# Sums of weights formed in the recurrence and read back, and a fourth pair with seven products, in a decoder layer

## The chip, the cores and the metric

The kernel runs on one core of one Trainium2 chip. A core has a matrix engine (TensorE, in the profile PE, with its weight loads shown as PEld), three engines that work on elements (VectorE or DVE, ScalarE or ACT, GpSimd or POOL), and DMA engines that move data between DRAM and the on-chip memory. DMAs are issued by the queues of engines, here mostly by SyncE (SP), which does nothing else. TensorE writes to a small accumulation memory (PSUM), from which the element engines read.

The metric is the device time of one execution in microseconds (us). Before the change the median of three runs is 2254.96 us.

## The reference: what is computed

The reference is one decoder layer in float32 for 256 tokens of width 2048. In order:

```python
x = x + 0.5 * swiglu(rms_norm(x, ffn1_norm), ffn1_w_gate, ffn1_w_up, ffn1_w_down)   # width 5632
x = gated_parallel_mixer(x, ...)      # attention with sinks, beside an RWKV-7 recurrence
x = memory_cross_attention(x, mem, ...)
x = x + 0.5 * swiglu(rms_norm(x, ffn2_norm), ffn2_w_gate, ffn2_w_up, ffn2_w_down)
return rms_norm(x, final_norm)

def swiglu(h, w_gate, w_up, w_down):
    return (silu(h @ w_gate) * (h @ w_up)) @ w_down
```

The mixer takes all its projections out of one product with `w_in`. Its recurrence has 16 heads of size 64 and is sequential over the tokens; the kernel computes it in blocks of 128 tokens, by chains of small matmuls. Most of the time goes into products of the 256 tokens with weights that are read once from DRAM, some 400 MB.

## The kernel before, in words

**Products.** A float32 matmul is made of three matmuls on rounded operands: each operand is split into a high part (a ScalarE cast, `hi`) and a low part (what is left, a VectorE subtraction, `lo`), and the products high x high, high x low and low x high are added (`times`, lines 409 to 414). The weights come in units of two 128-row blocks by 512 columns. `load` (line 316) issues a unit's DMA on SP's queue into a buffer `raw`, `split_unit` (line 333) splits it.

**Eight products or seven.** In the feed-forward layers (from the second 512 columns on) two weight blocks are taken together, gate and up of the same columns. Two token halves times two weights times two blocks of K, called a pair q, make a 2 x 2 by 2 x 2 product of blocks: eight block products of three matmuls each. For the pairs in `SEVEN` (0, 2 and 4 of the eight pairs) the kernel uses the known scheme with seven products (p1 to p7 in `product_pair`, line 472). It needs sums of the activations (`combinations`, line 424; tiles `chi`, `clo`; four sums for each such pair, two for a plain pair ahead of the last one) and four sums of the weights, formed by four VectorE subtractions of 128 x 512 in `divide` (lines 366 to 369) and written to two `raw` buffers; the other operands are blocks of the weights as they are, so that an item with sums has one whole gate unit, half an up unit and two tiles of sums to split (`two_parts`, line 343, tiles `thi` and `tlo`, one buffer each for a and b).

**The order of the work.** `weight_plan` lists all products; their units form a list of items, one for each two blocks of K. `next_item` (line 373) hands out items, issues loads some units ahead (`LOADED`), and splits up to two units ahead (`AHEAD`); so for the paired items one item ahead. Items 0 to 139 are the first feed-forward layer, 140 to 379 the mixer and the cross-attention, the rest the second feed-forward layer.

All that isn't a product with weights is written as generators in groups of `Interleave` (line 52): attention, element work (`ew`), chains of the recurrence (two at a time), norms. A `tick` lets each of a group's first generators go one step. The loop of products calls a tick after each token half, so two for an item. The chains start behind item 267 and run beside the products with the gates of the recurrence (items 268 to 299); the product with `w_proj_rwkv` (items 300 to 315) reads their result `yr`. Each instruction goes to its engine's queue, which is worked off in order. `tc.issue_after` holds an instruction behind another one of the same engine.

**Memory.** The mixer's tiles of 4 KB per partition share a ring of `N4 = 22` buffers under the tag `t4`. The second feed-forward layer reuses the same memory: its `raw2` buffers (four, of two units each) take the loads of weights, and the four `raw` buffers then take sums.

## Time and profile before

| | |
|---|---|
| median of three runs | 2254.96 us (2254.9 to 2255.55) |
| profiled execution, its own time | 2254.95 us |
| its span, first to last instruction | 2253.2 us |
| TensorE busy | 2237.3 us, 10617 matmuls |
| VectorE busy | 1775.7 us |
| ScalarE busy | 1223.1 us |
| moved by DMA | 432.48 MB, mean 192 GB/s |
| granted TensorE clock | 0.999 |

How to read it: the shares are of the whole span, over stages that differ. The views by stretch show busy times in a window of the span. A row of the groups names line, engine, operation, result and operands, then shape and count, busy time and mean duration of one, and after a bar the idle time of that engine just before them and what ended it. In the list of waits, a row gives who waited for whom, the total, how often, and the longest one. In the timeline a row is start, duration, engine, line, operation. Matmuls overlap, so that a row's duration isn't what it takes in the stream; the distance between starts is.

### The profile page before, as it was taken

The page shows a single profiled execution, that of the slowest core. Times are in us where ns is not written, and L with a number is a line of the kernel's source. Part 1 is how long each engine was busy: PE and PEld are TensorE (multiplying, and loading weights), DVE is VectorE, ACT ScalarE, POOL GpSimd, SP SyncE. Part 2 cuts the span into 40 slices and gives each one's busy share as a digit, 9 for nine tenths or more (in the row PEclk, how much of TensorE's full clock was granted, in tenths as well). Part 3 has the DMA queues.
Part 4 walks back from the last instruction along what each step waited for, and adds up shares of the span by engine and source line. Part 5 has one row for each costly group of instructions (what it writes and reads, how often), then busy time and mean ns, then how long its engine had stood idle before and what let it go on. Part 6 is the DMA issues. An engine that isn't in the chain of part 4 may idle for free.

```text
span 2253.2 us, 28023 instructions
## 1 busy us (share of the span) xinstructions
PE 2237.3 (99%) x10617; PEld 1838.2 (82%) x10617; DVE 1775.7 (79%) x2273; ACT 1223.1 (54%) x1593; POOL 134.0 (6%) x192
## 2 busy tenths in 40 slices
PE   9999999999999999999999999999999999999998
PEld 7888888888888877788888888888888888888886
DVE  7898988998989476887534566547999988998987
ACT  6555555555556467444444446556555555554554
POOL 1000000000001000301220040001000000000002
PEclk9999999999999999999999999999999999999999
DMA  7565565556556545676533586558565565555564
GB/s 263 187 205 198 195 205 202 191 191 217 190 189 206 163 139 150 206 223 206 161 84 88 178 256 229 191 159 277 183 216 193 189 219 190 188 208 202 188 207 147
DMA packets 219142, 432.48 MB, mean 192 GB/s; under 512 B 14107, under 2 KB 16384, under 8 KB 219008
## 3 DMA queue, kind: packets, MB, share of 16 engines
q1 hardware_dynamic: 210432, 404.78, 54.7%
q0 software_dynamic: 8112, 25.12, 3.6%
q8 instruction: 83, 1.36, 0.3%
q10 hardware_dynamic: 464, 0.79, 0.1%
q14 instruction: 51, 0.42, 0.1%
HBM read 417.56 MB, written 13.11 MB: 191 GB/s over the span
## 4 chain that ended last, share of the span: by engine, by line
PE 47%; DVE 2%; DMA 1%; issue 0%; ACT 0%; POOLq 0%; POOL 0%; DVEq 0%; ACTq 0%
PE acc L412 9%; PE acc L414 9%; PE acc L413 9%; PE mm L414 4%; PE mm L413 4%; PE mm L412 4%; PE mm L1237 1%; PE tr L600 1%; PE tr L413 1%; PE tr L414 1%; PE tr L412 1%; DVE lo L340 1%; PE tr L1173 0%; DMA raw<-in_w_out_dram 0%; PE tr L1225 0%
## 5 line engine op out<-in xcount | busy, mean ns | idle before, releaser
L340 DVE TENSOR_TENSOR lo<-raw,hi 128x1024 fp32r<-128x1024 f32 (+1 forms) x770 | 894.2, 1163 | 345.6 <-ACT hi L339 343.9
L339 ACT CAST hi<-raw 128x1024 fp32r<-128x1024 f32 (+1 forms) x770 | 759.7, 997 | 736.1 <-PE acc L414 527.3
L412 PE MATMUL acc<-hi,xhi 128*128 128x512 f32 (+1 forms) x1196 | 476.4, 399 | 1.9 <-ACT xhi L627 1.4
L413 PE MATMUL acc<-lo,xhi 128*128 128x512 f32 (+1 forms) x1196 | 464.5, 388 | 0.0
L414 PE MATMUL acc<-hi,xlo 128*128 128x512 f32 (+1 forms) x1196 | 464.2, 389 | 0.0
L412 PEld LDWEIGHTS acc<-hi,xhi 128*128 128x128 f32 x1196 | 225.0, 188 | 52.2 <-issue 5.0
L414 PEld LDWEIGHTS acc<-hi,xlo 128*128 128x128 f32 x1196 | 224.4, 188 | 47.0 <-DVE xlo L628 1.0
L413 PEld LDWEIGHTS acc<-lo,xhi 128*128 128x128 f32 x1196 | 224.9, 188 | 46.2 <-issue 3.2
L347 ACT CAST thi<-raw 128x1024 fp32r<-128x1024 f32 x172 | 179.0, 1051 | 62.4 <-DVE raw L368 48.4
L348 DVE TENSOR_TENSOR tlo<-raw,thi 128x1024 fp32r<-128x1024 f32 x172 | 208.6, 1222 | 0.7 <-ACT thi L347 0.4
L412 PE MATMUL mm<-hi,xhi 128*128 128x512 f32 x380 | 149.3, 393 | 0.0
L414 PE MATMUL mm<-hi,xlo 128*128 128x512 f32 x380 | 148.1, 390 | 0.0
L413 PE MATMUL mm<-lo,xhi 128*128 128x512 f32 x380 | 148.1, 390 | 0.0
L413 PE MATMUL acc<-lo,hhi 128*128 128x512 f32 x372 | 145.5, 391 | 0.8 <-DVE lo L340 0.8
L414 PE MATMUL acc<-hi,hlo 128*128 128x512 f32 x372 | 145.5, 391 | 0.0
L412 PE MATMUL acc<-hi,hhi 128*128 128x512 f32 x372 | 144.9, 390 | 0.0
L414 PEld LDWEIGHTS mm<-hi,xlo 128*128 128x128 f32 x380 | 71.3, 188 | 15.0
L413 PEld LDWEIGHTS mm<-lo,xhi 128*128 128x128 f32 x380 | 71.4, 188 | 14.5
L412 PEld LDWEIGHTS mm<-hi,xhi 128*128 128x128 f32 x380 | 71.4, 188 | 14.5
L413 PEld LDWEIGHTS acc<-lo,hhi 128*128 128x128 f32 x372 | 69.9, 188 | 15.4 <-DVE lo L340 1.2
L412 PEld LDWEIGHTS acc<-hi,hhi 128*128 128x128 f32 x372 | 69.9, 188 | 14.3
L414 PEld LDWEIGHTS acc<-hi,hlo 128*128 128x128 f32 x372 | 69.9, 188 | 13.9
(384 smaller groups left out, 3500.6 us busy)
## 6 DMA issues: line engine op xcount, KB each, us to landing
raw<-in_ffn_w_up_dram SPq DMA_DIRECT2D x88, 1024.0 KB, 5.5
raw<-in_ffn_w_down_dram SPq DMA_DIRECT2D x88, 1024.0 KB, 5.2
raw<-in_ffn_w_gate_dram SPq DMA_DIRECT2D x84, 1024.0 KB, 5.2
raw<-in_w_in_dram SPq DMA_DIRECT2D x136, 512.0 KB, 3.7
raw<-in_w_out_dram SPq DMA_DIRECT2D x32, 512.0 KB, 4.6
raw<-in_w_proj_attn_dram SPq DMA_DIRECT2D x16, 512.0 KB, 4.1
raw<-in_w_proj_rwkv_dram SPq DMA_DIRECT2D x16, 512.0 KB, 5.4
raw<-in_w_cross_kv_dram SPq DMA_DIRECT2D x16, 512.0 KB, 4.0
```

The source lines that it names most:

```text
L339: at["hi"] = act.copy(hi[:, s], raw[:, s])
L340: at["lo"] = dve.tensor_tensor(lo[:, s], raw[:, s], f32(hi[:, s]), ALU.subtract)
L347: act.copy(hi[:], v[:])
L348: dve.tensor_tensor(lo[:], v[:], f32(hi[:]), ALU.subtract)
L412: pe.matmul(o, xh, hi, start=first, stop=False, **how)
L413: pe.matmul(o, xh, lo, start=False, stop=False, **how)
L414: pe.matmul(o, xl, hi, start=False, stop=last, **how)
L600: pe.transpose(b[:, o : o + P], tok[:, t, col : col + P], ident[:])
L1237: pe.matmul(vb[:, (o + k) * P : (o + k + 1) * P][:, r], lhs(k, e), rhs[:, k, r], start=first and k + e == 0, stop=True, **ek,)
```

## The change

In gate and up of the second feed-forward layer (`last`), pair 1 is taken in the seven-product form too: `SEVEN_2 = (0, 1, 2, 4)`. The weight sums of pairs 1 and 2 (`STAGED`) are no longer formed there. They are formed during the mixer, 20 times (two pairs of the ten products j = 1 to 10), by a new generator `stage` in a group of its own, four at a time: it waits for its position (`STAGE_AT`, items 255, 259, 263 and then 17 positions from 267 to 286), loads the four weight blocks into two `t4` tiles on SP's queue, lets four ticks pass, forms the sums in place in two steps of two VectorE subtractions each, lets six ticks pass, and stores the two tiles to DRAM (`sums`), on SP's queue too. In the second layer `load_sums` reads them back into `raw` buffers, up to two items ahead, and `divide` splits them. Of the up units in staged pairs, the block that only entered the sums isn't loaded; for that, some loads are cut into pieces.

The ring `t4` has 24 buffers instead of 22. To make room, the constants `bdup` and `center` move from the constant pool into the mixer's, `keep` takes the place of `ups`, and a smaller tile fills the gap in the constant pool. In the second layer the activation sums `chi` and `clo` hold 18 blocks instead of 16.

```diff
-N4 = 22
+N4 = 24
...
+SEVEN_2, STAGED = (0, 1, 2, 4), (1, 2)
+STAGE_AT = [255, 259, 263] + [267 + 21 * n // 17 for n in range(17)]
...
-                yield (wg, wu), 0, KD, (j * 512, j * 512), SEVEN
+                yield (wg, wu), 0, KD, (j * 512, j * 512), SEVEN_2 if last else SEVEN
...
+    bg.group("stage", 4)
...
-    bdup = cpool.tile([P, 2, P], F32, name="bdup")[:, 0, :]
-    center = cpool.tile([P, P], F32, name="center")
+    cpool.tile([P, P], F32, name="shift")
...
-        ups = sp.tile([P, 2, P], F32, name="ups")[:, 0, :]
+        keep = sp.tile([P, 2, P], F32, name="keep")
+        ups = keep[:, 0, :]
...
+            for i in range(2):
+                q = (k - k0) // KU + i
+                if n == SEVEN_2 and q in STAGED:
+                    staged[len(items)] = len(staged)
+                items.append(((u + i, u + 2 + i), q in n))
+    raws, parts, summed = {}, {}, {}
+    first_unused = {items[i][0][1] for i in staged}
+    sums_d = dram.tile([len(staged), P, 4, 512], F32, name="sums")
...
+        if u in first_unused:
+            second = u + 1 in first_unused
+            pieces = [(slice(1, 2), nc.sync)] + [(slice(2 + second, 4), nc.sync)]
+            if not second:
+                pieces = ((slice(1, 4), nc.sync),)
+        elif u + 1 in first_unused and wide:
+            pieces = ((slice(0, 2), nc.sync), (slice(3, 4), nc.sync))
...
+    def load_sums(i):
+        if i not in staged or i in summed:
+            return
+        summed[i] = [
+            wp.tile([P, KU, 512], F32, tag="raw", name="raw", bufs=4) for _ in range(2)
+        ]
+        for e, t in enumerate(summed[i]):
+            nc.sync.dma_start(t[:], sums_d[staged[i], :, KU * e : KU * e + KU, :])
+
+    def stage(t4, i, n):
+        while at["item"] < STAGE_AT[n]:
+            yield
+        t = t4("su", (P, KU, 512)), t4("sg", (P, KU, 512))
+        for e, v in zip(t, items[i][0][::-1]):
+            w, k, c0, _ = units[v]
+            rows = slice(k * P, (k + KU) * P)
+            nc.sync.dma_start(e[:], w[rows, c0 : c0 + 512].rearrange("(a p) n -> p a n", p=P))
+        yield from idle(4)
+        u0, u1, g0, g1 = (e[:, c] for e in t for c in range(KU))
+        with tc.issue_after(at["lo"].ins):
+            dve.tensor_tensor(g0, u0, g0, ALU.subtract)
+            dve.tensor_tensor(u0, u1, u0, ALU.subtract)
+        yield
+        with tc.issue_after(at["lo"].ins):
+            dve.tensor_tensor(u1, u1, g0, ALU.subtract)
+            dve.tensor_tensor(g1, g1, u1, ALU.subtract)
+        yield from idle(6)
+        for c, e in enumerate(t):
+            nc.sync.dma_start(sums_d[n, :, KU * c : KU * c + KU, :], e[:])
...
-        rg, ru = raws[g], raws[u]
-        t = [wp.tile([P, KU, 512], F32, tag="raw", name="raw", bufs=4) for _ in range(2)]
-        dve.tensor_tensor(t[1][:, 0], ru[:, 0], rg[:, 0], ALU.subtract)
...
+        t = summed.get(i)
+        if t is None:
+            rg, ru = raws[g], raws[u]
+            t = [wp.tile([P, KU, 512], F32, tag="raw", name="raw", bufs=4) for _ in range(2)]
+            dve.tensor_tensor(t[1][:, 0], ru[:, 0], rg[:, 0], ALU.subtract)
...
+            load_sums(j)
             divide(j)
+        load_sums(i + 2)
         return parts[i]
...
+        for i, n in staged.items():
+            bg.spawn("stage", stage(t4, i, n))
```

More of the change, by code (lines that the diff above doesn't have):

```diff
@@ L206, in mixer_constants @@
         select(mask_l[:], ups, [[-1, P]], ALU.is_gt, 0.0, 0, 1)
+        bdup = sp.tile([P, P], F32, name="bdup")
+        center = sp.tile([P, P], F32, name="center")
         bdones = sp.tile([P, P], F32, name="bdones")
@@ L217, in mixer_constants @@
         pool.tensor_tensor(center[:], ident[:], bdmean[:], ALU.subtract)
-        keep = sp.tile([P, 2, P], F32, name="keep")
         pool.memset(keep[:], 1.0)
         pool.memset(keep[:, :, 0:1], 0.0)
-        return abias, mask3, mask_l, bdones, bdmean, keep
+        return abias, mask3, mask_l, bdup, center, bdones, bdmean, keep
     sinks = cpool.tile([P, 16], F32, name="sinks")
@@ L292, in decoder_layer @@
     junk_t = cpool.tile([P, 512], mybir.dt.bfloat16, name="junk")
-    plan, units, items, ends = [], [], [], []
+    plan, units, items, ends, staged = [], [], [], [], {}
     for entry in weight_plan(a):
@@ L311, in decoder_layer @@
             units += [(v, k + i, c, 512) for v, c in zip(w, c0) for i in (0, KU)]
-            items += [((u + i, u + 2 + i), (k - k0) // KU + i in n) for i in range(2)]
-    raws, parts = {}, {}
+            for i in range(2):
[6 more added lines that the diff above has]
+    sums_d = dram.tile([len(staged), P, 4, 512], F32, name="sums")
     at = {"item": 0, "product": 0, "pool": None}
@@ L422, in multiply, with combinations @@
             )
-    def combinations(sp, x: Act, seven, name, ready=lambda: True, early=True):
+    def combinations(sp, x: Act, seven, name, ready=lambda: True, early=True, n=0):
         pairs = [q for q in range(max(seven) + 1) if early or q in seven]
-        n = 12 if not early else sum(4 if q in seven else 2 for q in pairs)
+        n = n or sum(4 if q in seven else 2 for q in pairs)
         parts = [sp.tile([P, n, P], F32R, tag=name + e, name=name + e) for e in ("hi", "lo")]
@@ L663, in feed_forward @@
         c = combinations(
-            sp, norm.x, SEVEN, "c", lambda: norm.r is not None and at["item"] > begun + 4
+            sp, norm.x, SEVEN_2 if last else SEVEN, "c", lambda: norm.r is not None and at["item"] > begun + 4
         )
@@ L671, in feed_forward @@
             )
-            ch = combinations(sp, h, SEVEN_DOWN[nj < 4], "d", early=False)
+            ch = combinations(sp, h, SEVEN_DOWN[nj < 4], "d", early=False, n=12)
             def transposed(hb, c):
```

12 lines of the change are left out of this document (6 added, 6 removed).

## The prediction

> **What bounds the kernel now.** I read the page first (shares and slices), then busy time by stretch, then who waits for whom, then TensorE's instructions in order of time.
>
> ```profile
> span 2253.2 us, 28023 instructions
> PE 2237.3 (99%) x10617; PEld 1838.2 (82%) x10617; DVE 1775.7 (79%) x2273; ACT 1223.1 (54%) x1593; POOL 134.0 (6%) x192
> DMA  7565565556556545676533586558565565555564
> ...
> L347 ACT CAST thi<-raw 128x1024 fp32r<-128x1024 f32 x172 | 179.0, 1051 | 62.4 <-DVE raw L368 48.4
> ```
>
> TensorE is busy for 99% of the span; VectorE is second. The DMA digits dip to 2 and 3 in slices 20 to 22, where the recurrence's chains run. By stretch (columns: window, length, then busy time and count of PE, PEld, DVE, ACT, POOL, granted clock, DMA share, GB/s):
>
> ```profile
> 1060.00:1280.00 220.00, 218.63 (x1406) 184.30 (x1405) 104.40 (x124) 97.17 (x143) 40.03 (x63) 1.00 0.42 118
> 1280.00:1320.00 40.00, 40.00 (x182) 33.09 (x181) 21.41 (x20) 18.05 (x19) 6.61 (x8) 1.00 0.85 287
> 1560.00:1724.00 164.00, 164.00 (x740) 135.41 (x739) 146.31 (x191) 93.48 (x108) 0.00 (x0) 1.00 0.60 204
> 1797.00:1966.00 169.00, 169.00 (x759) 139.79 (x758) 150.00 (x183) 94.74 (x106) 0.00 (x0) 1.00 0.59 199
> 2051.00:2178.00 127.00, 126.91 (x568) 104.60 (x567) 110.03 (x132) 70.27 (x78) 2.17 (x4) 1.00 0.61 207
> ```
>
> The last three rows are the three stretches of the second feed-forward layer that hold gate and up. TensorE is busy in all of their 460 us but 0.09, at full clock, VectorE for 89% and 87%. So a matmul left out there is worth what it takes in the stream, provided that its operands stay ready. The first row is the recurrence: VectorE 47% busy, DMA 0.42. The second, right behind, is where DMA is densest: 0.85 at 287 GB/s, or 338 GB/s at a full share.
>
> **The change part by part.** *(1) The matmuls.* A pair of 128-row blocks of K takes 8 products of 3 matmuls in plain form, 7 in the form with sums. In gate and up of the second layer, pair 1 joins pairs 0, 2 and 4. What a product takes in the stream is seen from the starts of pairs 0, 1 and 2 of one such product:
>
> ```profile
> 1627.70 0.39 PE L412 MATMUL tr<-thi,chi 128*128 128x512 f32 x1
> ...
> 1632.46 0.39 PE L412 MATMUL acc<-hi,xhi 128*128 128x512 f32 x1
> ...
> 1637.90 0.39 PE L412 MATMUL tr<-thi,chi 128*128 128x512 f32 x1
> ```
>
> Pair 0 (21 matmuls) takes 4.76 us, pair 1 (24) 5.44. The difference, 0.68, is three matmuls at 0.227, not at the 0.39 that a row shows for one alone, since they overlap. Ten products (j = 1 to 10) lose 30 matmuls: 30 x 0.2267 = **6.80 us**, all on the path.
>
> The Trainium skill (TensorE: Matmul & The Clock Gate, section Back-to-back issue gap) gives about 131 ns for each 512-column matmul in a sustained stream; by it the part would be worth an estimated 3.9 us, 30 x 0.131, and the whole change about 2.4. The trace disagrees, with 227 ns in its own stream, and decides.
>
> *(2) VectorE, ScalarE and DMA in the second layer.* Rows by shape:
>
> ```profile
> L340 DVE TENSOR_TENSOR lo<-raw,hi 128x1024 fp32r<-128x1024 f32 x672 | 826.5, 1231 | 331.8 <-ACT hi L339 330.1
> L348 DVE TENSOR_TENSOR tlo<-raw,thi 128x1024 fp32r<-128x1024 f32 x172 | 208.6, 1222 | 0.7 <-ACT thi L347 0.4
> L340 DVE TENSOR_TENSOR lo<-raw,hi 128x512 fp32r<-128x512 f32 x90 | 61.8, 688 | 7.4 <-ACT hi L339 7.4
> L366 DVE TENSOR_TENSOR raw<-raw,raw 128x512 f32<-128x512 f32 x86 | 59.3, 689 | 20.8 <-DMA raw<-in_ffn_w_up_dram 19.5 <-DMA raw<-in_ffn_w_down_dram 0.8
> ```
>
> Pair 1 now splits one whole unit, half a unit and two sums (1.23 + 0.69 + 2 x 1.22 = 4.36) where it split two units (2.46): +1.90. Pair 2 no longer forms its four sums: -4 x 0.69 = -2.76. VectorE does 0.86 us less per product of some 42 us, so it doesn't become the bound by load. ScalarE gains two casts of 1.05 (the page's row above) and loses half a cast: about +1.6 on an engine at 57%. DMA loads 1.05 MB of sums for each of the two staged pairs and leaves out one 128-row block of up (0.26 MB): 2 x (1.05 - 0.26) = 1.6 MB per 42 us, +37 GB/s on 199 to 207, a share of about 0.71. Five more issues per product on SP are hidden: SP mostly waits for buffers. What is new is the order: pairs 0, 1 and 2 are now three in a row with sums, and the buffers of the split sums (thi and tlo, a and b) are single. The a pair is read by the first two products of an item and is free early. The b pair is read to the item's last product; then cast (1.05) and subtraction (1.22) run, 2.27, before the sixth product of the next item needs it, 5 x 0.68 = 3.40 later. So 1.13 us are to spare: cost 0, bounds 0 and what the second rival takes.
>
> The sums of pair 2 go into the buffers that pair 0's sums leave, so their load is issued when pair 0's second tlo ends. The latest case is
>
> ```profile
> 1667.18 2.35 DVE L348 TENSOR_TENSOR tlo<-raw,thi 128x1024 fp32r<-128x1024 f32 x2
> ...
> 1670.14 0.39 PE L412 MATMUL tr<-thi,chi 128*128 128x512 f32 x1
> ...
> DMA to landing us min/median/max: 5.0/5.2/8.1
> ```
>
> It ends 0.6 us before pair 0 starts. The last row is the landing time of this stretch's weight loads (1560 to 1724). Landing after 5.2 to 8.1 us is at 4.6 to 7.5 us into pair 0; pair 2 starts at 2 x 4.76 = 9.5 and needs its first cast and subtraction (2.27) by then, so 7.2. In time, but for the worst landing by 0.3: cost 0.
>
> *(3) The sums in the recurrence, VectorE.* 20 x 4 subtractions of 0.69 = 55 us more VectorE work. In 1060 to 1280 its share goes from 104.4 to 159 of 220, 0.72. Each half-step puts up to 1.4 us ahead of other VectorE work. The splits run two items ahead of TensorE and hide it. The masks of the chains don't:
>
> ```profile
> PE tr L1276 <- DVE mk L1179: 0.7, 2, 0.4
> PE tr L1322 <- ACT gr L1364: 0.3, 1, 0.3
> PE tr L1210 <- DVE mk L1179: 0.3, 1, 0.3
> ```
>
> TensorE's whole waits in 1060 to 1320 are these, 1.0 on masks. No row shows the price with the new work; bounds are 0 and one half-step before each of 12 mask steps, 16.6. I scale the waits with VectorE's load, 1.0 x 159/104 = 1.5: **+0.5**, near the lower end since the list of waits is nearest.
>
> *(4) The sums in the recurrence, DMA.* Each stage reads and writes 1.05 MB: at 338 GB/s 6.2 us of all DMA engines, 124 us for 20. From 1060 to 1280, 0.58 x 220 = 128 us are free. So it just fits if even, and it isn't even: four stages run at once, each for 12 ticks (6 items), so loads and stores come in fours, and the last store comes behind item 297, into the dense stretch. There:
>
> ```profile
> 1258.05 21.93 SPq L331 DMA_DIRECT2D raw<-in_w_in_dram  x7
> ...
> 1285.59 1.05 ACT L339 CAST hi<-raw 128x1024 fp32r<-128x1024 f32 x1 [1.81 <-DMA raw<-in_w_in_dram]
> ...
> DMA to landing us min/median/max: 4.5/5.8/8.8
> ```
>
> Seven weight loads (3.7 MB) go out in 21.9 us, and the cast at 1285.59 already waited 1.81 for a load; the last row is the landing time of the weights from 1276 to 1312. By the positions, five stores and a load of sums (6.3 MB) come among these seven. Both make 10 MB, 29.6 us of DMA in 22: weights land up to 8 us late. TensorE is covered by two items of 2.72 less 2.3 for cast and subtraction, about 3.1 us, and by earlier landing of all but the one load. Bounds 0 and 8 - 3.1 = 4.9. I take **+1.0**: today's late cast costs TensorE nothing, and a backlog partly drains before it. Earlier bursts are covered, because there the chains' matmuls stretch the items: the gate products' sigmoids run
>
> ```profile
> L1364 ACT ACTIVATE gr<-acc,rs x8: 681/687/690, 1182.9 to 1296.3; 128x512 f32<-128x512 f32 x8
> ...
> ACT hi L339 <- PE acc L414: 69.3, 47, 3.6
> ```
>
> from the end of the first product to that of the fourth, so 24 items take 113.4 us, 4.7 each; and from 1060 to 1320 the casts wait 47 times for TensorE to free a buffer, which means that the weights had landed.
>
> *(5) Buffers of the recurrence (t4).* The chains hold up to 20 to 22 of 22 around item 275; stages add up to 8, and two are added, so one or the other waits. Cover: the last low part of the chains' result ends at 1272.4, its first reader starts at 1296.1.
>
> ```profile
> L606 DVE TENSOR_TENSOR yrlo<-yq,yrhi x4: 683/685/692, 1182.2 to 1271.7; 128x512 fp32r<-128x512 f32 x4
> ...
> 1296.13 0.39 PE L412 MATMUL acc<-hi,yrhi 128*128 128x512 f32 x1
> ```
>
> Cost 0, as the chains may slip by 23 us while gate matmuls fill TensorE; the bound above is in the first rival. *(6) The rest.* Constants moved between pools, a shared tile for ups and keep, wider chi and clo (18 blocks for 16; two more 128-column sums once): POOL is 6% busy, the sums lie beside the plain product j = 0. 0.
>
> **Sum.** -6.80 + 0.5 + 1.0 = -5.3. The profiled execution took 2254.95 with a span of 2253.2, and the median of the runs is 2254.96, so the same sum holds against both: **2249.6 us**. What a measurement of this kernel tells from no change is about 0.2%, 4.5 us.
>
> **Rivals.** *First: the recurrence gives part of it back.* The backlog of (4) counts in full (+4.9) with the +0.5: 2254.95 - 6.8 + 5.4 = 2253.6, within 0.2%. If SP also stands before a t4 buffer, with all weights queued behind it, one such stand of three items at 4.7 us less the cover of 3.1 adds 11: 2264.6. For: DMA need 124 of 128 us. Against: weights lie ready for long in the chains' stretch. *Second, slower: the single b buffers.* If VectorE has two subtractions of 1.22 in hand when the cast of b ends, b is 2.44 late, 1.13 is to spare, and TensorE stands 1.31 at each of 20 staged pairs: 26 us, 2254.95 - 5.3 + 26 = 2276. It takes back the whole 5.3 from 0.27 us per pair on, thus from a delay of 1.4, a little over one subtraction. For: VectorE is at 89%. Against: TensorE has no wait at all there today, and VectorE loses load. *Third: a matmul left out gives back only its weight load,* as the stream may be paced by something else.
>
> ```profile
> L412 PEld LDWEIGHTS acc<-hi,xhi 128*128 128x128 f32 x1196 | 225.0, 188 | 52.2 <-issue 5.0
> ```
>
> 30 x 0.188 = 5.6, so 2254.95 - 5.6 + 1.5 = 2250.8, within 0.2%. The starts in (1) speak against it: pairs of 21 and 24 matmuls differ by three at 0.227. That the sums are formed but save no matmul is excluded by the plan of pairs.
>
> **How the numbers follow.** Forecast 0.58, between 2248.1 (nothing lost) and 2250.4. First rival 0.27: 0.22 within 0.2%, 0.05 slower. Second 0.13, slower. Third 0.02, same. So faster 0.58, same 0.24, slower 0.18. The range, 2247.6 to 2259.0, holds the first two signs and leaves out the slower ones; its low end is the full 6.8 and a little of the runs' spread (0.65).
>
> **What would show it.** Right: 30 matmuls fewer in the three gate-and-up stretches, each product 0.68 us shorter, PE without idle time; TensorE's waits in the recurrence 1 to 3 us instead of 1.3. Wrong: TensorE waiting for tlo (second rival), for lo or hi behind a late load around 1280 to 1300, or for masks (first), or SP's queue standing before a stage's buffer.

## The result: 0.14% slower, and the profile after

The changed kernel takes 2257.95 us (median of 20 runs, 2255.44 to 2261.81), the kernel before 2254.78 (20 runs on the same chips). The ratio is 1.0014, with an interval of 1.0008 to 1.002. The forecast was 2249.6; by its own bound of 0.2% this is hardly a change, but the interval lies on the slower side. The profiled execution took 2255.44, the fastest of the 20, so it shows less of the loss than a usual run has; a second profile, at 2257.95, comes below.

The page of the changed kernel:

```profile
span 2253.6 us, 28371 instructions
PE 2233.5 (99%) x10587; PEld 1834.6 (81%) x10587; DVE 1825.8 (81%) x2336; ACT 1241.1 (55%) x1613; POOL 132.8 (6%) x192
DMA  7555565556556544676988886547765666657664
```

There are 30 matmuls fewer (10587 for 10617), and TensorE is busy 3.8 us less, yet the span is 0.4 us longer. The dip to 3 in the DMA digits is filled with 8s. Busy time by stretch (window, length, then PE, PEld, DVE, ACT, POOL, granted clock, DMA share, GB/s); the last three rows are gate and up of the second feed-forward layer, the first of them at its new place:

```profile
1060.00:1280.00 220.00, 218.26 (x1398) 184.02 (x1397) 153.19 (x199) 95.81 (x142) 39.34 (x62) 1.00 0.87 293
1280.00:1320.00 40.00, 37.61 (x157) 30.01 (x157) 20.61 (x20) 15.81 (x16) 6.75 (x8) 0.96 0.92 321
1567.00:1731.00 164.00, 164.00 (x739) 135.01 (x738) 147.85 (x188) 100.71 (x115) 0.00 (x0) 1.00 0.67 233
1797.00:1966.00 169.00, 169.00 (x758) 139.82 (x757) 151.00 (x178) 101.90 (x115) 0.00 (x0) 1.00 0.68 239
2051.00:2178.00 127.00, 127.00 (x569) 104.92 (x568) 111.35 (x130) 76.84 (x85) 2.17 (x4) 1.00 0.71 242
```

In the later layer TensorE has no idle time. Pair 1 now takes as long as pair 0, as the starts of pairs 0, 1 and 2 in TensorE's timeline show (4.76 us apart each, where pair 1 took 5.44):

```profile
1592.00 0.39 PE L469 MATMUL tr<-thi,chi 128*128 128x512 f32 x1
...
1596.76 0.39 PE L469 MATMUL tr<-thi,chi 128*128 128x512 f32 x1
...
1601.52 0.39 PE L469 MATMUL tr<-thi,chi 128*128 128x512 f32 x1
```

Laying the starts of the same work in both traces side by side gives the ledger. The first gate product of the recurrence ends 1.63 us later than before, the second 1.81, the third 2.31, the fourth 6.44; the first product with sums of the later layer starts 6.77 later, and the last matmul 0.16 earlier (the 0.4 us of the span lie behind it). So the later layer gains 6.77 + 0.16 = 6.93 us, as forecast, and what lies before it takes all of it back: 6.44 in the recurrence, 4.13 of them between the third and the fourth gate product, and 0.33 behind it. TensorE's waits from 1060 to 1320:

```profile
PE acc L469 <- ACT hi L392: 2.4, 1, 2.4
PE tr L1336 <- DVE mk L1239: 0.7, 2, 0.4
PE tr L657 <- DVE mk L1239: 0.5, 1, 0.5
PE tr L1270 <- DVE mk L1239: 0.3, 1, 0.3
PE tr L1382 <- DVE mk L1239: 0.2, 1, 0.2
```

The third row is where the first 1.63 us come about. Up to 1127 us TensorE's matmuls start within 0.4 us of before, from 1142 on some 1.6 later. In between VectorE makes a mask of the chains, in its timeline before the change and after:

```profile
1125.84 1.28 DVE L1179 TENSOR_TENSOR mk<-tr,mask 128x512 f32<-128x512 f32 x2
```

```profile
1129.70 1.29 DVE L1239 TENSOR_TENSOR mk<-tr,mask 128x512 f32<-128x512 f32 x2 [0.76 <-DMA sums<-sg]
```

Four subtractions of a stage (1126.07 to 1128.9) stand ahead of the mask in VectorE's queue. Behind them VectorE is idle for 0.76 us, until a store of sums has landed: the masks take their tiles from the ring `t4` too, and the mask starts 0.1 us after that landing.

The first row is new: one wait of 2.4 us for the cast of a weight. The cast of this weight (item 296) in ScalarE's timeline, with the idle time ahead of it and what ended it in brackets:

```profile
1288.69 1.04 ACT L392 CAST hi<-raw 128x1024 fp32r<-128x1024 f32 x1 [7.46 <-DMA raw<-in_w_in_dram]
```

and the matmuls on both sides of the wait in TensorE's:

```profile
1287.04 0.39 PE L471 MATMUL acc<-hi,xlo 128*128 128x512 f32 x1
1289.79 1.22 PE L469 MATMUL acc<-hi,xhi 128*128 128x512 f32 x2 [2.36 <-ACT hi L392]
```

ScalarE had been idle for 7.46 us when the weight landed. What SP's queue did before (start, duration; L351 are weight loads, L384 stores of sums):

```profile
1265.18 0.38 SPq L351 DMA_DIRECT2D raw<-in_w_in_dram  x1
1271.45 0.32 SPq L384 DMA_DIRECT2D sums<-su  x1
1272.65 0.32 SPq L384 DMA_DIRECT2D sums<-sg  x1
1273.06 0.40 SPq L351 DMA_DIRECT2D raw<-in_w_in_dram  x1
1279.06 0.32 SPq L384 DMA_DIRECT2D sums<-su  x1
1279.78 0.41 SPq L384 DMA_DIRECT2D sums<-sg  x1
1280.61 3.74 SPq L351 DMA_DIRECT2D raw<-in_w_in_dram  x3
```

and its waits from 1040 to 1320:

```profile
SPq L351 <- DVE lo L393: 135.0, 50, 9.8
SPq L384 <- DVE su L380: 40.6, 17, 5.9
SPq L384 <- DVE sg L381: 11.5, 14, 2.1
```

Twice SP stands for some 6 us before a store, because VectorE has not yet formed the sum (rows two and three: 52 us of such standing in all), and the weight loads stand behind it. Item 296 was issued at 1280.6 instead of 1271.8, 8.8 us later: 4.3 because the buffer that it reuses came free late (the `lo` subtraction of item 292 ended at 1276.1 instead of 1271.8; 1.8 of this is the delay that the recurrence had by then, since the cast of item 292 starts 1.8 later), 4.5 because SP stood. It then took 8.0 us to land instead of 3.9, among the stages' bytes.

After the wait the matmuls themselves are slow. The granted clock (third number from the right) in three short stretches:

```profile
1286.00:1290.00 4.00, 1.64 (x8) 1.05 (x7) 0.23 (x1) 1.04 (x1) 0.00 (x0) 0.96 1.02 345
1290.00:1294.00 4.00, 3.96 (x11) 2.69 (x12) 3.44 (x3) 2.09 (x2) 0.00 (x0) 0.61 1.03 412
1294.00:1298.00 4.00, 4.00 (x19) 3.32 (x18) 1.23 (x1) 1.47 (x2) 0.00 (x0) 1.00 0.99 363
```

In the middle row 11 matmuls run in 4 us where 19 do in the last. So the 4.13 us are 2.36 of waiting and some 1.8 behind it, most of it the lower clock.

To read the experiments, one more quantity is needed, the *lead* of a weight: from its landing to the start of its cast. Worked out from the issue, landing and cast of every weight in the traces (us; 0.1 means that the cast waits for the landing):

```
item                 240   255   268   270   276   288   292   294   296   298
before               2.7   5.3   6.5  10.9  29.9  22.0  12.0   8.5   4.3   0.1
changed kernel       3.8   4.5   0.1   7.0  26.5  22.4   6.5   1.4   0.1   0.1
```

Already before the change, weights lead by some 3 to 8 us up to item 269, by 10 to 30 only from item 270 (its load is issued at 1103 us) to 293 (1258 us), while the chains' matmuls stretch the items, and behind them by less and less, down to 0.1 at item 298. The changed kernel's stages start at items 255 to 291 and their last stores go out behind the load of item 298. A lead of 0.1 isn't yet a wait of TensorE, since the cast runs ahead of it: item 268 has this lead after the change, and costs TensorE nothing.

### The profile page after: what moved, and what is told of

Read it like the earlier page. It is cut to its first block, busy times and chain, and to the rows that moved or that the text cites. A ratio compares the mean times of both kernels' runs of the same rounds, so it can differ in the third digit from the quotient of the medians.

```text
span 2253.6 us, 28371 instructions
## 1 busy us (share of the span) xinstructions
PE 2233.5 (99%) x10587; PEld 1834.6 (81%) x10587; DVE 1825.8 (81%) x2336; ACT 1241.1 (55%) x1613; POOL 132.8 (6%) x192
## 4 chain that ended last, share of the span: by engine, by line
PE 46%; DMA 2%; DVE 1%; issue 1%; ACT 0%; POOLq 0%; POOL 0%; SPq 0%; DVEq 0%; ACTq 0%
PE acc L469 9%; PE acc L470 9%; PE acc L471 9%; PE mm L471 4%; PE mm L470 4%; PE mm L469 4%; PE tr L657 1%; DMA raw<-in_w_in_dram 1%; PE tr L470 1%; PE tr L469 1%; PE tr L471 1%; PE mm L1297 1%; DMA raw<-in_w_out_dram 0%; PE tr L1233 0%; DVE lo L393 0%
## 5 line engine op out<-in xcount | busy, mean ns | idle before, releaser
L469 PE MATMUL acc<-hi,xhi 128*128 128x512 f32 (+1 forms) x1166 | 464.6, 400 | 4.8 <-ACT hi L392 2.4
L470 PE MATMUL acc<-lo,xhi 128*128 128x512 f32 (+1 forms) x1166 | 453.9, 389 | 0.0
L471 PE MATMUL acc<-hi,xlo 128*128 128x512 f32 (+1 forms) x1166 | 452.9, 389 | 0.0
L469 PEld LDWEIGHTS acc<-hi,xhi 128*128 128x128 f32 x1166 | 219.7, 189 | 54.5 <-issue 5.3
L470 PEld LDWEIGHTS acc<-lo,xhi 128*128 128x128 f32 x1166 | 219.6, 188 | 45.6 <-issue 3.2
L471 PEld LDWEIGHTS acc<-hi,xlo 128*128 128x128 f32 x1166 | 219.2, 188 | 45.5 <-DVE xlo L685 1.0
L401 DVE TENSOR_TENSOR tlo<-raw,thi 128x1024 fp32r<-128x1024 f32 x192 | 232.9, 1222 | 3.5 <-ACT thi L400 0.4
L400 ACT CAST thi<-raw 128x1024 fp32r<-128x1024 f32 x192 | 200.1, 1051 | 60.5 <-DVE raw L423 36.4
```

Of the source, the lines that this page charges most:

```text
L400: act.copy(hi[:], v[:])
L401: dve.tensor_tensor(lo[:], v[:], f32(hi[:]), ALU.subtract)
L469: pe.matmul(o, xh, hi, start=first, stop=False, **how)
L470: pe.matmul(o, xh, lo, start=False, stop=False, **how)
L471: pe.matmul(o, xl, hi, start=False, stop=last, **how)
```

## The experiments

Times are medians; ratios are against runs of the kernel before on the same chip (2254.48 to 2255.01). In what follows "loss by the fourth gate product" and "gain of the later layer" are differences of starts in the profiled execution, as in the ledger above (6.44 and 6.93).

**The fourth pair without the stages.** No sums go through DRAM; the later layer forms all of them.

```diff
-SEVEN_2, STAGED = (0, 1, 2, 4), (1, 2)
+SEVEN_2, STAGED = (0, 1, 2, 4), ()
```

> Pair 1 is a seven-product pair, but nothing is formed in the recurrence: the sums of pairs 1 and 2 are formed in the second feed-forward layer. Theory (all that the change loses is lost in the recurrence): the recurrence is as before the change, and the layer gains up to 6.8 us, so 2248 us if VectorE keeps up. Rival (the sums had to leave the layer): VectorE there gets 1.9 + 2.8 us more per product of 42 us, from 89% to about 100%, TensorE waits for lo or tlo at each of the ten products, and the time is 2252 us or more.

2266.79 us, ratio 1.0052 (1.0039 to 1.0064). The loss by the fourth gate product is 0.04: without stages the recurrence is as before. Another 2.9 us are lost between it and the later layer, at one wait that comes up again below, and the later layer gets 9.40 us longer. Its middle stretch by busy time:

```profile
1797.00:1966.00 169.00, 163.72 (x725) 132.55 (x724) 162.36 (x202) 98.51 (x111) 0.00 (x0) 1.00 0.57 197
```

and the first of TensorE's waits from 1545 on:

```profile
PE tr L469 <- ACT thi L400: 11.0, 11, 1.4
```

VectorE is at 162.36 of 169, and TensorE stands for the sums. The subtractions have to leave this layer for the fourth pair to be worth anything.

**The stages without the fourth pair.** The sums are formed and stored, and never read; the later layer is as before.

```diff
-                yield (wg, wu), 0, KD, (j * 512, j * 512), SEVEN_2 if last else SEVEN
+                yield (wg, wu), 0, KD, (j * 512, j * 512), SEVEN
...
-                if n == SEVEN_2 and q in STAGED:
+                if len(ends) == 2 and n == SEVEN and q in STAGED:
```

> The sums are formed in the recurrence and stored, but never read; the second feed-forward layer is as before the change. Theory: the whole cost of the change lies in the recurrence, so this is slower than before by what the changed kernel lost there, 6.9 us in its profiled execution and some 9 to 10 us by its median: 2262 to 2265 us. Rival (part of the loss comes from reading the sums back, or from the memory's new layout): 2258 us or less.

2264.69, ratio 1.0043 (1.0029 to 1.0057), a loss of 9.7 us; 7.02 by the fourth gate product in the profile (2262.39, again the fastest of its runs). This is the price of the stages alone, in the memory's new layout, and its median exceeds its profile as the changed kernel's does.

**Stores on POOL's queue.**

```diff
-            nc.sync.dma_start(sums_d[n, :, KU * c : KU * c + KU, :], e[:])
+            pool.dma_start(sums_d[n, :, KU * c : KU * c + KU, :], e[:])
```

> The changed kernel, but the 40 stores of sums are issued by GpSimd's queue instead of SP's; the same bytes move at the same places. Queue theory (SP stands before stores that wait for VectorE, and the weights of items 294 to 300 queue behind it): TensorE's wait of 2.4 us around 1287 goes, with the slow clock behind it, some 4 us in the profiled execution and more in the median: 2251 to 2253 us. Bandwidth theory (the 16 DMA engines are full from 1260 to 1300 whoever issues): no change, 2257 to 2258 us.

2256.41 (2253.21 to 2262.47), ratio 1.0008 (0.9999 to 1.0017). Only 1.5 us of the median comes back. In its profile the wait at item 296 is gone, but the first gate product ends 3.48 us late. Now POOL stands before the stores, 99 us in all from 1040 to 1320, and TensorE waits 1.4 us for the mask of the chains that it waits 0.5 for in the changed kernel; VectorE is idle for 1.7 us before this mask, until a store of sums has landed. The stages alone, with the stores on SP's queue, have this wait at 1.2, so that it isn't the move's alone.

```profile
PE tr L657 <- DVE mk L1239: 1.4, 1, 1.4
PE tr L1336 <- DVE mk L1239: 0.7, 2, 0.4
PE acc L469 <- ACT gr L1424: 0.6, 1, 0.6
```

The Trainium skill (Trainium Kernel Development and Optimization, section Key Constraints) says that DMAs from the queues of SP, ACT and POOL run on the same 16 DMA engines, so that issuing from several saves only issue time. The DMA side agrees: from 1260 to 1300 the DMA engines are as full as in the changed kernel (0.98 at 360 GB/s there), and VectorE is as busy (29.91 there). What the move changed was which engine's queue stands, and TensorE is busy for all 40 us:

```profile
1260.00:1300.00 40.00, 40.00 (x189) 32.63 (x188) 30.93 (x36) 16.98 (x20) 7.57 (x13) 1.00 1.03 385
```

**Ten stages instead of twenty**, one pair only, one start each three items.

```diff
-SEVEN_2, STAGED = (0, 1, 2, 4), (1, 2)
+SEVEN_2, STAGED = (0, 1, 2, 4), (1,)
-STAGE_AT = [255, 259, 263] + [267 + 21 * n // 17 for n in range(17)]
+STAGE_AT = [258 + 3 * n for n in range(10)]
```

> Only the sums of pair 1 are formed in the recurrence, ten stages three items apart from item 258 on; those of pair 2 are formed in the layer as before the change. Bandwidth and queue theories both: half the transfers, never more than two stages at once, so the wait around 1287 goes: loss in the recurrence 1 to 2 us, and with 6.8 us gained 2249 to 2250 us, unless VectorE, with 1.9 us more per product (89% to 93%), falls behind in the layer: then 2252 us or more with waits for lo or tlo there.

2251.8, ratio 0.9986 (0.9978 to 0.9995): faster than both kernels. The loss by the fourth gate product falls to 0.47, the gain of the later layer to 4.19. Half of the stages cost a fourteenth of the loss, so the price is not one per stage. The later layer pays with VectorE near its limit again:

```profile
1797.00:1966.00 169.00, 168.74 (x752) 138.33 (x751) 157.43 (x194) 102.44 (x115) 0.00 (x0) 1.00 0.62 213
```

With 22 `t4` buffers instead of 24 the same version takes 2251.53 (ratio 0.9985, 0.9977 to 0.9994).

> The version with ten stages (2251.8) with 22 t4 buffers as before the change instead of 24. Theory: with 24 the fourth x2 load is no longer held by a t4 buffer and meets the w_out weights, which cost 0.6 us there; with 22 it is held again, 2251.2, unless stages then wait for t4 buffers and hold SP: then 2252 or more.

Between the recurrence and the later layer it loses 0.28 us instead of 0.63: with 24 buffers the fourth load of `x2` no longer waits for a buffer and goes out 36 us earlier (1352.8 instead of 1388.9), among the weights of `w_out`. The runs of the two versions overlap, so that this rests on the traces. Other profiles with 24 buffers lose more at this place: 2.9 us without the stages and 2.8 in the profile without subtractions below, each with one wait of TensorE for `x` (1.8 and 1.7 us, at 1369) and a granted clock of 0.91 from 1360 to 1380. So this price of the memory's new layout varies, and it is there without any stage.

**VectorE or the stores?** Two versions of the stages alone (2264.69), whose output doesn't depend on them: one stores the loaded weights instead of sums, with no subtraction; the other forms the sums and stores nothing.

```diff
-        with tc.issue_after(at["lo"].ins):
-            dve.tensor_tensor(g0, u0, g0, ALU.subtract)
-            dve.tensor_tensor(u0, u1, u0, ALU.subtract)
...
-        for c, e in enumerate(t):
-            nc.sync.dma_start(sums_d[n, :, KU * c : KU * c + KU, :], e[:])
```

> The stage-only version (sums made and stored, never read, FFN2 as before; 2264.69) without VectorE's four subtractions per stage: what is stored is the loaded weights, not sums. Bytes and queues are the same, but nothing of it uses VectorE and no store waits for VectorE. Theory A1 (bandwidth of the DMA engines alone): the loss of 9.7 us stays, 2262 to 2265. Theory A2 (SP standing before stores that wait for VectorE, and VectorE itself late): most of it goes, 2255.5 to 2258.

> The stage-only version without the stores: loads and VectorE's subtractions stay, the sums go nowhere. Theory A1 (bandwidth): half of the bytes go, and with them more than half of the loss: 2256 to 2259. Theory A2a (SP standing before stores): the same, 2256 to 2258, but the DMA share in 1100 to 1300 us would be beside the point. Theory A2b (VectorE late by the subtractions, so that the lo splits release the weight buffers late): the loss stays at 5 us or more, above 2260. With the version without VectorE it makes a square of two causes.

2255.74 (ratio 1.0006, 0.9997 to 1.0014) and 2255.99 (1.0005, 0.9996 to 1.0014): either removal takes away nine tenths of the loss. (The profile without subtractions is the slowest of its 11 runs, 2258.2; it loses 0.59 by the fourth gate product.) The stretch from 1260 to 1300 without subtractions, and without stores:

```profile
1260.00:1300.00 40.00, 40.00 (x175) 32.80 (x176) 21.91 (x20) 20.07 (x23) 3.56 (x5) 1.00 0.96 356
```

```profile
1260.00:1300.00 40.00, 40.00 (x175) 32.81 (x176) 30.73 (x35) 20.00 (x23) 4.28 (x6) 1.00 0.77 261
```

The first has the DMA engines as full as the changed kernel's (0.98 at 360 GB/s there), the second VectorE as busy (29.91 there), and neither loses anything there: TensorE is busy for all 40 us. Without subtractions item 296 is issued at 1272.4, lands after 7.6 us, and leads by 0.5. So neither full DMA engines alone nor a busy VectorE alone makes this wait. But both versions also end SP's standing before the stores: one has no sum to wait for, the other no store to issue. The version with the stores on POOL's queue ends only that, has both the full DMA engines and the busy VectorE, and doesn't have the wait either: it loses 1.39 us between the third and the fourth gate product instead of 4.13. So at item 296 SP's standing is a part that the wait needs; how the rest is shared between VectorE and the DMA engines these versions don't tell.

**When the stores go out.** This was meant to show that SP's standing is the cause of the whole loss: six more idle steps ahead of the stores, so that the sums are ready when SP comes to them; or four fewer.

```diff
-        yield from idle(6)
+        yield from idle(12)        # and idle(2) in the other
         for c, e in enumerate(t):
```

> The changed kernel with the two stores of a stage six half-items later (12 idle steps after the subtractions instead of 6), so that the sums are done when SP reaches their stores. Bytes, subtractions and buffers are the same. Theory A2 (what costs is SP standing before stores that wait for VectorE, with the weight loads queued behind it): the waits of L384 for VectorE go, the wait at item 296 goes, the recurrence loses about 1 us instead of 6.9, and the time is 2249 to 2251. Theory A1 (DMA bandwidth): no better than 2256.

> The dose the other way: stores 2 idle steps after the subtractions instead of 6. Theory A2: SP's waits of L384 for VectorE grow from 52 us to some 90 or more, more weights come late, 2261 or more. Theory A1: bytes are the same, 2256 to 2259.

Both came out the other way: 2272.12 with the late stores (ratio 1.0082, 1.0069 to 1.0095), 2252.84 with the early ones (0.9992, 0.9984 to 1.0001). The standing itself went as planned, 17.5 us of waits of L384 for VectorE instead of 52 with late stores, and 68 with early ones; the time went against it. So the account by the sum of SP's standing falls. It isn't a clean test of the standing at item 296, since both versions also move the stages' end: from 1260 to 1300 SP waits for VectorE before stores for 14.3 us in the changed kernel, for 8.1 with early stores, which end at 1271 instead of 1285, and not at all with late ones, which go on to 1345. What the late stores do is move the stages' end, since only four run at once and each lasts longer. Late stores, by stretch, and TensorE's waits:

```profile
1260.00:1300.00 40.00, 34.62 (x154) 27.30 (x152) 26.25 (x32) 13.92 (x16) 2.16 (x3) 0.96 0.90 313
1300.00:1340.00 40.00, 30.69 (x119) 22.04 (x120) 25.82 (x31) 13.18 (x16) 6.70 (x7) 0.94 1.04 398
```

```profile
PE acc L469 <- ACT hi L392: 6.6, 4, 3.5
PE acc L470 <- DVE lo L393: 2.3, 4, 0.8
```

From 1300 to 1340 the DMA engines had been 0.85 busy before the change; now they are full, and TensorE runs 119 matmuls where 190 ran before. Early stores end the stages sooner: in that version TensorE's wait at item 296 is gone and the loss by the fourth gate product is 1.64.

Late stores with 22 buffers:

> The late stores with 22 t4 buffers instead of 24. If SP does not stand before a stage's buffer, the fourth x2 load is held as before the change and 0.3 to 0.6 us is gained on the late stores alone; if it does (two buffers fewer, each held 3 items longer), SP's waits of the stage loads for t4 readers grow from some 5 us to 20 or more and the time is 2 us or more above that of the late stores alone.

2270.4 (ratio 1.0073, 1.0061 to 1.0085), 1.7 below those with 24, and SP's longest wait for a `t4` reader is 3.7 us: stages hardly stand for buffers.

**Another place for ten of the stages.** Five at items 176 to 192, ten in the chains' stretch as in the version with ten, five at items 326 to 364.

```diff
-STAGE_AT = [255, 259, 263] + [267 + 21 * n // 17 for n in range(17)]
+STAGE_AT = [176 + 4 * n for n in range(5)] + [258 + 3 * n for n in range(10)] + [326, 349, 354, 359, 364]
```

> All 20 stages and both staged pairs as in the changed kernel, but the stages begin at items 176 to 192 (five), 258 to 285 in steps of three (ten) and 326 to 364 (five). Theory A (the loss comes from crowding: up to four stages at once beside the chains fill the DMA engines and hold SP, and one wait at item 296 is the largest part): the recurrence loses what the half version lost there, about 1 us, the later layer gains the full 6.9, so about 2249. Theory B (each stage has a price of its own wherever it lies, 6.9 us / 20 = 0.35 us in the profiled run): no better than the changed kernel, about 2258.

2254.53, ratio 0.9999 (0.999 to 1.0008). The wait at item 296 is gone, and the later layer gains 6.40; but the first five cost 0.95 us before the chains begin, and 4.57 are lost between the fourth gate product and the later layer, where the last five lie. Of these, 3.5 come about at the wait for `x` around 1370 (2.3 us here), where other versions with 24 buffers lose up to 2.9 without a stage there; what the last five cost by themselves isn't shown.

**All stages 12 items earlier.** If the loss came only from the end of the chains, this would heal it.

```diff
+STAGE_AT = [243, 247, 251] + [255 + 21 * n // 17 for n in range(17)]
```

> The changed kernel with every stage begun 12 items earlier (243 to 274 instead of 255 to 286), so that the last stores lie near item 285 instead of 297. Theory C (late weights cost only where the chains no longer hold the items: the lead of a weight load over its use is 20 us at items 288 to 290, 4 us at 296, 0 at 298; stage work that ends ahead of item 288 costs only what it takes from the chains): no wait at item 296, the recurrence loses 2 to 2.5 us by its last gate instead of 6.4, and the time is 2250.5 to 2252. Theory D (the number of stages at once, and the full DMA engines, cost the same wherever in the recurrence they lie): 2256 or more. SP standing before t4 buffers (16 to 18 of the others are in use at items 236 to 245) would add 1 to 3 us in either.

2275.09, ratio 1.0088 (1.0074 to 1.0101): a miss, and the slowest of all. The end is clean: item 296 leads by 4.7 us. But the first gate product already ends 27 us late. By stretch, and TensorE's waits:

```profile
1060.00:1100.00 40.00, 38.36 (x182) 31.17 (x181) 33.13 (x43) 16.65 (x20) 7.52 (x8) 1.00 1.04 393
1100.00:1140.00 40.00, 31.32 (x153) 23.07 (x151) 23.26 (x32) 9.88 (x14) 11.71 (x18) 0.87 1.02 339
1140.00:1180.00 40.00, 39.22 (x224) 31.99 (x223) 24.37 (x35) 12.93 (x20) 3.48 (x5) 0.83 0.74 261
```

```profile
PE acc L469 <- ACT hi L392: 7.3, 4, 5.3
PE acc L470 <- DVE lo L393: 3.1, 5, 0.8
```

The stages now run through items 251 to 269, where weights led by only 3 to 8 us before the change: all of them land late (leads of 0.1 to 2.1), the chains' first mask comes 19.8 us late, and the mean clock falls to 0.87 and 0.83 in two stretches of 40 us. The list of direct waits, 10.4 us, is well under the 27 lost; the rest runs at the lower clock or in gaps that the list doesn't count.

**Seventeen stages spread evenly** from item 252 to 285, 22 buffers; three of the second pair's sums are formed in the later layer.

```diff
+                if n == SEVEN_2 and q in STAGED and (q == 1 or len(staged) % 5 != 2):
+STAGE_AT = [252 + 33 * n // 16 for n in range(17)]
```

> 17 of the 20 sums (all of the first staged pair, seven of ten of the second), begun evenly from item 252 to 285, with 22 t4 buffers; three products of the later layer form their sums on VectorE as before. Theory C: the stages lie thinner, one per two items, but the last stores reach item 291 and more: a small wait near 296, some 1.5 us lost in the recurrence; the later layer gains 5.5 to 6.5 of 6.9: 2249.5 to 2251.5, level with ten stages (2251.5) or better. Theory D: the loss is in proportion to the stages, 17/20 of the changed kernel's: 2255 to 2257.

2262.14, ratio 1.0033 (1.0021 to 1.0046), a miss too. All of the loss, 13.9 us, has come about by the first gate product: one stage each two items ahead of item 270 is more than the leads there bear (items 259 to 269 land with 0.1). Behind it nothing is lost.

**Only the stretch with leads.** Two versions with 16 sums (all ten of one pair, six of the other). The first is the changed kernel without its last four stages; the second, with 22 buffers, has two single stages ahead of item 268 and 14 from 268 to 286.

```diff
+                if n == SEVEN_2 and q in STAGED and (q == 1 or len(staged) % 3 != 2):
...
+STAGE_AT = [255, 259, 263] + [267 + 21 * n // 17 for n in range(13)]
...
+STAGE_AT = [258, 264] + [268 + 18 * n // 13 for n in range(14)]
```

> The changed kernel with its first 16 stages at their places and without the last four (four products of the later layer form their sums on VectorE as before). Theory C (a stage costs where the lead of the weights is small, so the last four, at 1235 to 1284 us, make the wait at item 296): no wait there, the recurrence loses the 1.8 to 2.3 us that the changed kernel has lost by its second and third gate products, instead of 6.4; the later layer keeps 5 to 6 of 6.9: 2251 to 2252.5. Theory D (a price per stage): 16/20 of 6.4 in the recurrence is lost, 2254 or more.

> 16 sums, none begun between items 264 and 268 nor after 286: two alone at items 258 and 264, 14 from 268 to 286, where a weight load lands 10 to 30 us ahead of its use; 22 t4 buffers. Theory C: the early burst of the changed kernel (item 268 lands with no lead, 1.6 us) and the wait at item 296 both go; the recurrence loses 0.5 to 1.5 us: 2249.5 to 2251.5, the fastest of the versions. If stages then end too late again (last store beyond item 294), the wait at 296 is back and it is 2253 or more.

2253.46 (ratio 0.9994, 0.9985 to 1.0003) and 2250.93 (0.9983, 0.9975 to 0.9992). From 1260 to 1300, and all of TensorE's waits from 1060 to 1320, without the last four stages:

```profile
1260.00:1300.00 40.00, 40.00 (x189) 32.78 (x188) 21.73 (x21) 19.33 (x22) 2.42 (x4) 1.00 0.67 219
```

```profile
PE tr L657 <- DVE mk L1239: 1.1, 1, 1.1
PE tr L1336 <- DVE mk L1239: 0.7, 2, 0.4
PE tr L1270 <- DVE mk L1239: 0.3, 1, 0.3
PE tr L1382 <- DVE mk L1239: 0.2, 1, 0.2
```

The wait of 2.4 us and the slow clock are gone, and the loss by the fourth gate product is 2.42 instead of 6.44; 2.22 of it have come about by the first, at the mask of the first row, for which TensorE waits 1.1 us here. The last four stages alone cost 4.0 us, and bring 6.93 - 4.64 = 2.3 in the later layer. Sixteen inside the stretch lose 1.72 and gain 5.20. This is the fastest version, 3.9 us below the kernel before, though its runs overlap those of the ten stages with 22 buffers.

**The changed kernel once more**, for a second profile.

> The changed kernel once more, for a second profile: its first profiled execution (2255.44) was the fastest of 20 and the median is 2257.95. If the rest is clock (mean granted clock 0.999 to 0.998 in the runs at 2255.4 to 2256.7, 0.996 in those at 2259.9 to 2261.8), the extra time lies behind waits in the recurrence, in stretches with a granted clock under 1.00; if it is longer waits, in the same place at a clock of 1.00.

2257.95, the median's own value. Against the first profile it loses 0.92 us more by the fourth gate product (7.36; the same wait, 2.3 us, at the same place), 0.5 more up to the later layer (its wait for `x` at 1375 is 1.2 us instead of 0.8), and gains 5.90 there instead of 6.93. Over the 20 runs the time goes with the mean granted clock: 0.998 and 0.999 in the four below 2257, 0.996 in the three highest, 2259.88 to 2261.81; a thousandth of the clock is 2.3 us. So part of the spread is clock and part small losses in several places; why one execution gets more of them than another stays open.

## Why the prediction was wrong

*(1), the matmuls,* and *(2), the later layer,* were right. Thirty matmuls fewer gave 6.93 us for 6.80 forecast (5.90 in the second profile), each pair 1 0.68 shorter, TensorE without idle time, no wait for `tlo`. With that the second rival, the single b buffers, is out, and so is the third, the weight load's price: 6.93 / 30 = 0.231 us for one matmul, and 0.227 by the starts. The 131 ns of the Trainium skill's page (TensorE: Matmul & The Clock Gate, section Back-to-back issue gap) would have given an estimated 3.9, and the trace disagrees after the change as before.

*(3), VectorE and the masks,* was near in TensorE's waits: 1.7 us for masks instead of 1.0, where +0.5 was forecast. But the wait of 0.5 at one mask goes with a loss of 1.63 by the first gate product, so that pricing waits at their length was too little. And it missed a second effect. A late VectorE doesn't only hold masks, it frees the weight buffers late (4.3 us for item 296) and holds SP before the stores (4.5). The step said that splits run two items ahead of TensorE and hide VectorE's load; what it left out is who waits for VectorE behind them.

*(4), the DMA in the recurrence,* is the step that failed. It was put at +1.0, with 4.9 as the upper bound; by the changed kernel's own trace the recurrence lost 6.44, of which 4.13 lie at the place that the prediction named, and the stages alone cost 9.7 in the median. So the sum of -6.80 + 0.5 + 1.0 became -6.93 + 1.63 + 0.68 + 4.13 + 0.33 in this trace (the later layer, then the delays by the first, third and fourth gate product and from there to the later layer). Two things were wrong in step (4). It took a backlog of bytes as the only delay, and the cover as 3.1 us, two items of matmuls less cast and subtraction. The lead of the weights could be read from the trace of before, and falls from 22 us at item 288 to 4.3 at 296 and 0.1 at 298; against it stand 8.8 us of later issue plus 4.1 of longer landing. And it priced a wait at its length, where the lower clock behind 2.36 us of waiting cost nearly as much again. That the earlier bursts are covered held in the changed kernel's trace, where no weight makes TensorE wait up to 1127 us; but an average of 4.7 us an item doesn't show it. The leads are 3 to 8 us up to item 269, and with more stages there 13.9 and 27 us were lost. (The DMA digits that it started from dip to 3, not to 2 and 3; nothing hangs on this.)

*(5), the buffers,* was put at nothing, and that was wrong too. It looked at SP, which stands little before a stage's buffer (3.7 us in its longest wait for a reader) and long before stores (52). It left out that the masks take buffers of the same ring: one waits until a store of sums has landed, in the changed kernel 0.76 us, in its second profile 1.0, in that of the stages alone 1.5, with 1.63, 1.96 and 2.35 lost by the first gate product. With early stores 1.47 are lost without such a wait, so the buffer isn't the greater part. The side effect of two more buffers, the early `x2` load, was not foreseen; it is part of the 0.33 us that the changed kernel loses between the fourth gate product and the later layer.

The first rival, at 0.27, was the right one in kind: the recurrence gives the gain back. Its form with a full backlog, 2253.6, is 4.4 below the median; that with SP standing, 2264.6, named the wrong thing that SP stands before. The measured time lies inside the range, 2247.6 to 2259.0, and on the other side of the time before than forecast; that it lies inside is luck as far as the sum goes, whose terms (3) to (5) make 1.5 us where the trace has 6.77.

What the runs show as the cause: stage work costs where weights have little lead, and where a mask of the chains comes behind it. Twenty stages of 2.1 MB need 124 of the 128 us of free DMA time, and the stretch where weights lead by over 10 us, 1103 to 1258, is shorter than the one that this was counted over. Shown by undoing are the last four stages (4.0 us), the subtractions and the stores (some 9 of 9.7 us each), SP's standing at item 296 (the stores on POOL's queue, in one profile), and the place (2275 with the stages earlier, 2272 with late stores, 2250.93 with 16 stages inside). Still open are the shares of VectorE and the DMA engines, and how the remaining 1.7 us of the best version come about.

## What to carry to other kernels

Before work is put beside other work, list for each load how long it lies ready before its use: an idle DMA share says where bytes fit, the lead says where a delay is free, and the two stretches need not be the same. A queue that issues both prefetches and stores passes on every wait of the stores to the prefetches, and moving the stores to another queue moves the wait there. When two changes each remove nearly all of a loss, look for what both removals have in common before calling it a matter of both together. Here both also took SP's standing away, and a version that took only that away lost the wait at item 296 too. And a store out of a ring of buffers holds its buffer until it has landed: whoever takes the next tile from the ring, a mask of the chains here, waits for it (0.76 us in the changed kernel).

## What the runs showed of the hardware that was not expected

A single gap lowers TensorE's clock: 2.75 us between the starts of two matmuls (1287.04 and 1289.79) were followed by a granted clock of 0.61 from 1290 to 1294, and of 1.00 in the 4 us after that. In the version without the stages a wait of 1.8 us was enough (0.51 from 1369 to 1372), while its waits of up to 1.4 us from 1797 to 1966 left the clock at 1.00. The traces don't give a shortest gap: with 17 stages, a wait of 1.4 us with one of 0.8 close behind it was followed by 0.50 from 1122 to 1125. The Trainium skill (TensorE: Matmul & The Clock Gate, section HAM oscillation — how this bites in real kernels) gives gaps of over some 3.4 us as what to avoid; here shorter ones were enough. Where gaps follow one another, as with the stages 12 items earlier, the mean clock is 0.87 and 0.83 in two stretches of 40 us.

A full DMA share is not one rate: from 318 GB/s (1100 to 1140 in the version without subtractions, share 1.01) to 412 (1290 to 1294 in the changed kernel, share 1.03). The estimate of 338 GB/s at a full share stood inside this.
